# Router logits from the rows themselves, an unsplit first gather, power on GpSimd, twelve load buffers and later second parts of splits

## The chip, the core and the metric

One core of a Trainium2 chip runs one launch of the kernel. The metric is the device time of that launch in microseconds. TensorE (PE) multiplies matrices, VectorE (DVE) and ScalarE (ACT) do elementwise work, GpSimd (POOL) does a little of it, and SyncE (SP) issues the loads. Each engine takes its instructions in the order in which the program lists them and waits on semaphores where data is not ready.

## What is computed

Two layers over 256 tokens of width 1024. Each layer has a token-mixing half (a gated recurrence beside differential attention) and a channel-mixing half: a dense SwiGLU in layer 0, eight experts with two per token in layer 1.

```python
for l in range(2):
    sh1, sc1, g1, sh2, sc2, g2 = split(silu(c) @ ada_w[l] + ada_b[l])
    h = rmsnorm(x, ln1_g[l]) * (1 + sc1) + sh1
    z = h @ w_in[l]
    lru = rg_lru(causal_conv(xr), ...) * gelu(yr)
    att = diff_attention(q, k, v, positions, ...)
    x = x + g1 * (concat([lru, att]) @ w_out[l])
    h = rmsnorm(x, ln2_g[l]) * (1 + sc2) + sh2
    x = x + g2 * (swiglu(h) if l == 0 else moe(h))      # moe: top 2 of 8 by h @ router
return rmsnorm(x, final_g)
```

All of it is float32. Weights are some 420 MB, read once.

## The kernel before

The weights are one stream of chunks of 128x2048 floats (1 MB). `want` and its relatives (L98, L992 to L1021) list the stream; `fetch` (L110) issues the load of the next chunk on SP at the place where the program first needs it. SP runs ahead of the other engines, so a load starts when its buffer is free. There are 10 rotating buffers and, in the experts, `raw2` as an eleventh. For the first 12 expert chunks there is a twelfth, made of two halves from the tags `eh` and `el` (L120).

A product in full precision is made of three fast ones. `split_next` (L138) takes half a chunk, a piece of 128x1024, and makes `wh` (ACT, rounded, L147) and `wl` (DVE, the rest, L148). `refill` (L167) keeps four pieces ready; `quarter` (L158) is one step of work on one piece: `tick()`, `refill()`, then the piece's matmuls. `tick` (L182) is the hand-written order of everything else: `after(n, fn)` puts `fn` n ticks later, in front of that tick's `refill`. `TICKS` (L67) holds the tick of each step of the mixing halves: `setup` (preparation of angles, masks and recurrence constants, L207 on), `scan` and `out` (`lru_scan`, L712; `lru_out`, L728), softmax steps and so on.

In layer 0 `mix_start` (L1047) begins with `queries_keys` (L591), eight quarters, one for each block k of the input; their matmuls are L599 (with `wh`) and L602 (with `wl`). Blocks come in pairs: `prepare_quarter` (L1082) makes a pair ready and lifts `limit`, which lets the next two pieces be split. Setup steps are due at ticks 3, 4, 5, 5, 6 and 11.

The inverse root of the mean square is made by DVE alone from a first guess in integer arithmetic and three Newton steps: `rsqrt` (L476) for the heads, `inv_rms` (L508) for rows, `inv_rms_all` (L1745) at the end.

During the dense half, `ada_sums` (L362) adds up the conditioning rows of layer 1 on DVE, into tiles that POOL clears and gives the bias (`ada_bias`, L372); `ada_row` (L380) sums them over partitions and ACT copies the result.

`route` (L1305) norms both row tiles, transposes them, applies gain and shift, forms the logits, takes the best two, ranks the tokens of each expert and starts the first gather. `gather` (L1451) collects the tokens of an expert by matmuls with 0/1 matrices; it reads normed rows split into `xh` and `xl`. Then experts run by load: places 0 to 2 (j = 0, 2, 3 of the loop in `experts`, L1616) hold up to 128 tokens and use split weights (`glu_unit`, L845), places 3 and 4 (j = 5, 6) up to 96 (`glu_mid`, L921) and the rest (j = 1, 4, 7) up to 64 (`glu_half`, L880); the last two kinds multiply raw chunks in float32 without a split. `scatter` (L1564) brings the results of a large expert back.

Of the kernel before, what the change touches and what calls it, by code (L numbers as in the profile page):

```python
# [39 lines left out]
SCATTER = [1, 1, 1, 6, 1, 1, 5, 2, 2, 2, 2]  # L40
# [22 lines left out]
SHORT = 12  # L63
# [3 lines left out]
TICKS = [{"setup": [3, 4, 5, 5, 6, 11], "steps": STEPS, "rk": [9, 10], "rq": [10, 10], "tk": [10, 11], "tq": [12, 12], "s": [12, 14, 16, 17], "conv": [13, 13], "gate": [14, 15], "decay": 16, "scan": 19, "gelu": 19, "out": [20, 21], "v": 21, "att": [22, 24], "norm": [23, 27], "ada": [12, 12, 12, 15, 15, 16, 19, 19, 20], "fill": [0, 4, 4]}, {"setup": [1, 3, 3, 7, 7, 8, 10], "steps": STEPS, "rk": [9, 9], "rq": [10, 11], "tk": [10, 10], "tq": [11, 12], "s": [12, 14, 16, 17], "conv": [11, 13], "gate": [14, 15], "decay": 16, "scan": 19, "gelu": 19, "out": [20, 21], "v": 21, "att": [22, 24], "norm": [23, 31], "ada": [7, 9, 10, 10, 15, 15, 16, 17, 18], "fill": [1, 1, 3]}]  # L67
# [8 lines left out]
class Kernel:  # L76
    def __init__(self, ctx, tc, a):
# [10 lines left out]
        self.spos = 0  # L88
        self.ready = []
# [20 lines left out]
    def fetch(self):  # L110
# [3 lines left out]
        n = RAW_BUFS + (2 if 0 <= i < SHORT else 1)  # L114
        more = (i if i < SHORT else i - SHORT) % n - RAW_BUFS if i >= 0 else -1
# [3 lines left out]
        else:  # L119
            e[1] = [self.moe.tile([P, PIECE], F32, tag=tag, name="raw", bufs=3) for tag in ("eh", "el")]  # L120
# [86 lines left out]
    def setup(self):  # L207
# [21 lines left out]
        nc.gpsimd.memset(self.ones, 1.0)  # L229
        self.csil = const.tile([P, NK], F32, name="csil")  # L230
# [131 lines left out]
    def ada_sums(self, l, g, half, acc):  # L362
        nc = self.nc
        for i in range(NK if half is None else 4):
            raw = self.load(self.a["ada"][l, g, i // 2 + (0 if half is None else 2 * half), i % 2])
            for j in range(2):
                src = raw[:, j * 1024:(j + 1) * 1024]
                k, out = (i, acc[:, j * 1024:(j + 1) * 1024]) if half is None else (2 * i + j, acc)
                nc.vector.scalar_tensor_tensor(out, src, self.csil[:, k:k + 1], out, op0=ALU.mult, op1=ALU.add)
                yield  # L370

    def ada_bias(self, l, g, half, n, tag):  # L372

        acc = self.work.tile([P, 4 * n], F32, tag=tag, name="sums")
# [133 lines left out]
    def inv_rms(self, *ts):  # L508
# [5 lines left out]
        for t, (v, k, y, u) in zip(ts, r):  # L514
            ss = self.ss[t]
            nc.vector.tensor_scalar(v[:, 0:1], ss[:, 0:1], ss[:, 1:2], D * EPS, op0=ALU.add, op1=ALU.add)
# [1433 lines left out]
```

## Time and profile before

| | us |
|---|---|
| median of 3 runs | 1282.72 |
| lowest, highest | 1280.12, 1283.36 |
| profiled execution | 1281.7 |
| its span on the core | 1279.7 |
| busy: PE, DVE, ACT, POOL | 1225.4, 706.1, 553.7, 15.1 |
| moved by DMA | 424.68 MB, mean 332 GB/s |

The page gives shares over the whole span. The kernel goes through stages that differ in what limits them, so the rows below are taken from single stages: windows of time with the busy time of each engine and the rate of the loads, the chain of work that ended last, and the timeline of a few microseconds.

### The profile page before, as it was taken

What the parts mean: (1) busy time and instruction counts of PE and PEld (TensorE: products, weight loads), DVE (VectorE), ACT (ScalarE), POOL (GpSimd) and SP (SyncE); (2) the same over time, 40 slices, a digit from 0 to 9 for tenths busy, and PEclk for the clock granted to TensorE, in tenths of its full rate; (3) what the DMA queues carried; (4) which work ended last, traced back from release to release, by engine and by line L of the source; (5) the groups of instructions that cost most, each with busy time, mean ns of one, the idle gap of its engine ahead of it and who ended that gap; (6) DMA issues with size and microseconds to landing.
All of it is one profiled execution on the core that took longest, in us unless ns stands there. A gap on an engine that the chain in (4) does not pass through costs nothing.

```text
span 1279.7 us, 19448 instructions
## 1 busy us (share of the span) xinstructions
PE 1225.4 (96%) x7702; PEld 810.8 (63%) x7702; DVE 706.1 (55%) x1095; ACT 553.7 (43%) x812; POOL 15.1 (1%) x28
## 2 busy tenths in 40 slices
PE   6999999999999899999998999999999999999994
PEld 5777799999978678788434888888433333333331
DVE  4878778776577768889205988999301001000102
ACT  3475444444455937788104787777110000010001
POOL 0000100000000000000000000000000000000000
PEclk9999999999999998999999999999999999999998
DMA  9985878887454257889899999999899999799993
GB/s 378 425 353 184 319 259 328 304 303 279 164 218 161 100 197 283 298 335 351 356 427 427 426 426 380 354 352 370 350 426 427 425 413 415 300 377 376 426 427 154
DMA packets 60147, 424.68 MB, mean 332 GB/s; under 512 B 7394, under 2 KB 7658, under 8 KB 8848
## 3 DMA queue, kind: packets, MB, share of 16 engines
q1 hardware_dynamic: 59760, 423.28, 83.5%
q8 instruction: 62, 1.02, 0.3%
q14 instruction: 37, 0.30, 0.1%
q0 software_dynamic: 288, 0.09, 0.0%
HBM read 422.29 MB, written 1.05 MB: 331 GB/s over the span
## 4 chain that ended last, share of the span: by engine, by line
PE 60%; DMA 4%; DVE 4%; ACT 2%; issue 1%; DVEq 0%; ACTq 0%; SPq 0%
PE gps L895 4%; PE ups L895 4%; PE yps L987 3%; PE gps L948 3%; PE ups L948 3%; PE bps L960 3%; PE yps L917 3%; DMA raw<-i_md 3%; PE yps L203 3%; PE yps L202 3%; PE yps L204 3%; PE gps L203 3%; PE gps L204 2%; PE gps L202 2%; PE ups L204 2%; PE ups L202 2%
## 5 line engine op out<-in xcount | busy, mean ns | idle before, releaser
L148 DVE TENSOR_TENSOR wl<-raw,wh 128x1024 fp32r<-128x1024 f32 x344 | 411.4, 1221 | 92.6 <-ACT wh L147 89.2
L147 ACT ACTIVATE wh<-raw 128x1024 fp32r<-128x1024 f32 x344 | 358.9, 1059 | 148.9 <-PE gps L586 46.2
L586 PE MATMUL gps<-hl,wh 128*128 128x256 f32 x384 | 96.5, 283 | 0.7 <-DVE hl L572 0.7
L584 PE MATMUL gps<-hh,wh 128*128 128x256 f32 x384 | 96.6, 284 | 0.4 <-DVE hh L571 0.4
L586 PEld LDWEIGHTS gps<-hl,wh 128*128 128x128 f32 x384 | 73.6, 192 | 1.3 <-DVE hl L572 1.1
L584 PEld LDWEIGHTS gps<-hh,wh 128*128 128x128 f32 x384 | 73.6, 192 | 0.8 <-DVE hh L571 0.6
L906 DVE TENSOR_TENSOR sgs<-sgs,ups 128x512 f32<-128x512 f32 x9 | 6.2, 689 | 121.5 <-PE ups L895 121.5
L917 PE MATMUL yps<-raw,hTs 128*64 128x512 f32 x288 | 68.2, 597 | 4.2 <-DMA raw<-i_md 4.2
L953 DVE TENSOR_TENSOR sgm<-sgm,ups 128x512 f32<-128x512 f32 x6 | 4.1, 688 | 116.7 <-PE ups L948 116.7
L895 PE MATMUL ups<-raw,ef 128*64 128x512 f32 x288 | 65.5, 595 | 1.5 <-DMA raw<-i_mu 1.5
L895 PE MATMUL gps<-raw,ef 128*64 128x512 f32 x288 | 66.3, 598 | 0.0
L588 PE MATMUL gps<-hh,wl 128*128 128x256 f32 x384 | 61.7, 283 | 0.0
L203 PE MATMUL gps<-wl,eh 128*128 128x512 f32 x144 | 57.1, 396 | 2.3 <-DVE wl L148 2.3
L202 PE MATMUL yps<-wh,fh 128*128 128x512 f32 x144 | 58.3, 405 | 0.0
L202 PE MATMUL gps<-wh,eh 128*128 128x512 f32 x144 | 57.3, 398 | 0.0
L202 PE MATMUL ups<-wh,eh 128*128 128x512 f32 x144 | 57.2, 397 | 0.0
L203 PE MATMUL yps<-wl,fh 128*128 128x512 f32 x144 | 57.1, 396 | 0.0
L203 PE MATMUL ups<-wl,eh 128*128 128x512 f32 x144 | 57.0, 396 | 0.0
L204 PE MATMUL gps<-wh,el 128*128 128x512 f32 x144 | 57.0, 396 | 0.0
L204 PE MATMUL ups<-wh,el 128*128 128x512 f32 x144 | 57.0, 395 | 0.0
L204 PE MATMUL yps<-wh,fl 128*128 128x512 f32 x144 | 56.7, 394 | 0.0
L588 PEld LDWEIGHTS gps<-hh,wl 128*128 128x128 f32 x384 | 53.0, 192 | 0.0
(336 smaller groups left out, 2046.3 us busy)
## 6 DMA issues: line engine op xcount, KB each, us to landing
raw<-i_mu SPq DMA_DIRECT2D x96, 1024.0 KB, 8.9
raw<-i_md SPq DMA_DIRECT2D x96, 1024.0 KB, 10.2
raw<-i_mg SPq DMA_DIRECT2D x95, 1024.0 KB, 8.6
raw<-i_ada SPq DMA_DIRECT2D x48, 1024.0 KB, 6.8
raw<-i_win SPq DMA_DIRECT2D x20, 1024.0 KB, 10.2
raw<-i_fg SPq DMA_DIRECT2D x12, 1024.0 KB, 6.5
raw<-i_fu SPq DMA_DIRECT2D x12, 1024.0 KB, 5.5
raw<-i_fd SPq DMA_DIRECT2D x12, 1024.0 KB, 5.1
```

Source lines behind the costliest of these rows:

```text
L147: nc.scalar.activation(wh, raw, AF.Copy)
L148: self.rests.append(lambda: nc.vector.tensor_tensor(wl, raw, wh.bitcast(F32), op=ALU.subtract))
L202: mm(out, lhsT=xh, rhs=wh, start=start, stop=False)
L203: mm(out, lhsT=xh, rhs=wl, start=False, stop=False)
L204: mm(out, lhsT=xl, rhs=wh, start=False, stop=stop)
L584: self.nc.tensor.matmul(out, lhsT=w, rhs=hh[:, k, :], stop=False, start=k == 0 and (len(ks) == NK or m + j == 0))
L586: self.nc.tensor.matmul(out, lhsT=w, rhs=hl[:, k, :], start=False, stop=False)
L588: self.nc.tensor.matmul(out, lhsT=wl[:, j * len(ks) + i, :], rhs=hh[:, k, :], start=False, stop=k == NK - 1 and (len(ks) == NK or m + j == 1))
L895: nc.tensor.matmul(ps[c * HALF:(c + 1) * HALF, :], lhsT=eh[:, k, :], rhs=w[c][i // 2][:, i % 2, :], start=k == 0, stop=k == NK - 1)
L917: self.nc.tensor.matmul(y[n * HALF:(n + 1) * HALF, :], lhsT=hT[:, b, c * HALF:(c + 1) * HALF], rhs=w[n][b // 2][:, b % 2, :], start=i == 0 ...
L948: nc.tensor.matmul(ps[q(2 * c + s), :], lhsT=eh[:, k, q(s)], rhs=ws[w][c][i // 2][:, i % 2, :], start=k == 0, stop=k == NK - 1)
L960: nc.tensor.matmul(bp[q(2 * w + c), :], lhsT=eh[:, k, q(2)], rhs=ws[w][c][i // 2][:, i % 2, :], start=k == 0, stop=k == NK - 1)
```

## The change

Nine things are changed.

1. Layer 1's router: the rows of x are transposed as they are, without the norm; the logits are products of these with router times gain, then scaled by the inverse root and shifted by a row worked out earlier (`router_row`). The first gather reads the normed rows in float32, unsplit, 128 columns wide; `xh` and `xl` are made two and three ticks later. Two of the four conditioning loads in `route` are moved to ticks 1 and 2, the addition to tick 3.
2. Each inverse root: a power of -0.5 on GpSimd and one Newton step.
3. In the experts all chunks go round 12 buffers; the twelfth is a half `raw3` and the tile `xn1` of `core`. The tag `xn` with two buffers becomes two tags, `xn0` and `xn1`; `el` goes from three buffers to two.
4. `refill` issues `wh` of a new piece, then `wl` of the pieces that earlier calls left over; `piece` issues it if it is still missing.
5. `ada_bias` is gone: the first term of each sum writes instead of adding, the bias comes with `mod_row` at tick 20, and `ada_row` adds on DVE instead of copying on ACT.
6. In both layers `"out": [20, 21]` becomes `"out": [19, 21]` in `TICKS`.
7. `SCATTER` has other ticks, and `scatter` handles one half of the columns after the other.
8. `mhalf`, a constant of -0.5, is written at the start on POOL.
9. The cleared half of the slot matrix in `route` is no longer needed.

```diff
-SCATTER = [1, 1, 1, 6, 1, 1, 5, 2, 2, 2, 2]
+SCATTER = [1, 1, 1, 3, 2, 2, 1, 1, 3, 2, 2]
...
-        n = RAW_BUFS + (2 if 0 <= i < SHORT else 1)
-        more = (i if i < SHORT else i - SHORT) % n - RAW_BUFS if i >= 0 else -1
+        more = i % (RAW_BUFS + 2) - RAW_BUFS if i >= 0 else -1
...
-            e[1] = [self.moe.tile([P, PIECE], F32, tag=tag, name="raw", bufs=3) for tag in ("eh", "el")]
+            e[1] = [self.moe.tile([P, PIECE], F32, tag="raw3", name="raw", bufs=1),
+                    self.core.tile([P, PIECE], F32, tag="xn1", name="raw")]
...
     def piece(self, n):
+        if len(self.rests) >= len(self.ready):
+            self.split_rest()
         return [w.rearrange("p (a b) -> p a b", a=n) for w in self.ready.pop(0)]
 
     def refill(self, most=1 + AHEAD):
+
+        old = len(self.rests)
         while len(self.ready) < most and self.spos < self.limit and self.split_at(self.spos * PIECE // RAW):
-            self.split_next()
+            self.split_next(False)
+        for _ in range(old):
+            self.split_rest()
...
-        nc.scalar.activation(row, ps, AF.Copy)
+        nc.vector.tensor_tensor(row, ps, row, op=ALU.add)
...
         for t in ts:
-            r.append([self.small.tile([P, 3], F32, tag=f"iv{t}", name="iv")]
-                     + [self.small.tile([P, 1], d, tag=f"i{n}{t}", name=n) for n, d in zip("kyu", (I32, F32, F32))])
...
+            nc.vector.tensor_scalar(v, ss[:, 0:1], ss[:, 1:2], D * EPS, op0=ALU.add, op1=ALU.add)
+        for v, y, u in r:
+            nc.gpsimd.tensor_tensor(y, v, self.mhalf[:, 0:v.shape[-1]], op=ALU.pow)
+        for v, y, u in r:
+            nc.vector.scalar_tensor_tensor(u, y, y, v, op0=ALU.mult, op1=ALU.mult)
+        for v, y, u in r:
+            nc.vector.scalar_tensor_tensor(y, u, 3.0, y, op0=ALU.subtract, op1=ALU.mult)
+        return [y for v, y, u in r]
...
+        def best(t, y):
+            nc.vector.scalar_tensor_tensor(lg[:, t, :], lps[t], y, self.rbias, op0=ALU.mult, op1=ALU.add)
+            nc.vector.max(top[:, t, :], lg[:, t, :])
+            nc.vector.max_index(idx[:, t, :], top[:, t, :], lg[:, t, :])
+            nc.vector.tensor_copy(idf[:, t, :], idx[:, t, 0:2])
...
+        self.flip(banks, self.x[:, 0, :], 0, 0)
+        run(2)
+        self.flip(banks, self.x[:, 1, :], 1, 0)
+        for i in range(4):
+            copy(0, i, False)
+        for i in range(4):
+            copy(1, i, i % 2)
+        y, = self.inv_rms(1)
+        logits(0)
+        logits(1)
...
+        def parts(t):
+            nc.scalar.activation(xh[t], out[t], AF.Copy)
+            nc.vector.tensor_tensor(xl[t], out[t], xh[t].bitcast(F32), op=ALU.subtract)
+
+        for t in range(NT):
+            self.after(2 + t, lambda t=t: parts(t))
...
-        self.after(1, lambda: gate2(1))
+        for n in range(3):
+            self.after(1 + n, lambda: run(1))
```

## Rows read from the trace of the kernel before

**Rows 1.** Windows: busy us of PE, PEld, DVE, ACT, POOL; clock, DMA share, GB/s.
```profile
760.00:860.00 100.00, 100.00 (x447) 80.86 (x446) 92.87 (x90) 79.25 (x89) 0.00 (x0) 1.00 0.97 368
```
**Rows 2.** Windows of ten microseconds where loads start to follow without a break.
```profile
610.00:620.00 10.00, 10.00 (x47) 4.64 (x48) 2.31 (x4) 1.01 (x2) 0.00 (x0) 1.00 0.61 228
620.00:630.00 10.00, 10.00 (x46) 3.21 (x42) 1.94 (x3) 1.12 (x2) 0.00 (x0) 1.00 1.01 426
...
1150.00:1160.00 10.00, 10.00 (x98) 2.96 (x90) 0.18 (x1) 0.60 (x1) 0.00 (x0) 1.00 0.63 236
```
**Rows 3.** The chain that ended last: start, us, what.
```profile
496.78 5.15 PE gaps L1489 x32
...
663.52 19.04 DMA raw<-i_md
...
1238.51 19.52 DMA raw<-i_md
```
**Rows 4.** Timeline of layer 0's first projection: start, us, engine, line, output<-inputs.
```profile
27.62 2.36 DVE L148 TENSOR_TENSOR wl<-raw,wh 128x1024 fp32r<-128x1024 f32 x2
...
29.73 1.07 PE L602 MATMUL zps<-wl,hh 128*128 128x512 f32 x4
...
29.90 0.16 DVE L252 CAST set<-set 128x2 f32<-128x2 int32 x1
...
33.97 0.28 DVE L405 TENSOR_TENSOR row<-adaps,row 128x128 f32<-128x128 f32 x1
...
34.30 0.39 PE L412 MATMUL colps<-cst,row 128*128 128x4 f32 x2 [1.03 <-DVE row L405]
...
38.19 2.35 DVE L148 TENSOR_TENSOR wl<-raw,wh 128x1024 fp32r<-128x1024 f32 x2
...
39.46 1.20 PE L602 MATMUL zps<-wl,hh 128*128 128x512 f32 x4
...
42.70 0.07 DVE L301 MEMSET set<- 128x8 f32 x1
```
**Rows 5.** Timeline where layer 0's output product begins.
```profile
108.00 1.20 DVE L148 TENSOR_TENSOR wl<-raw,wh 128x1024 fp32r<-128x1024 f32 x1
...
110.92 0.79 PE L202 MATMUL wops<-wh,hh 128*128 128x512 f32 x1 [2.72 <-DVE hh L571]
...
111.51 0.63 PE L203 MATMUL wops<-wl,hh 128*128 128x512 f32 x1
```
**Rows 6.** Timeline: POOL's work, and an inverse root on DVE from first to last.
```profile
34.41 0.10 POOL L666 MEMSET xr<- 128x12 f32 x1 [30.55 <-ACT sincos L270]
...
150.87 1.35 DVE L536 TENSOR_SCALAR xn<-x,y 128x1024 f32<-128x1024 f32 x1
...
485.38 0.21 DVE L516 TENSOR_SCALAR iv<-ss 128x1 f32<-128x1 f32 x1 [0.19 <-ACT junk L505]
...
487.36 0.75 DVE L536 TENSOR_SCALAR xn<-x,y 128x1024 f32<-128x1024 f32 x1
...
1264.61 2.50 POOL L1768 TENSOR_TENSOR o<-x,fg 128x512 f32<-128x512 f32 x2 [68.33 <-DVE x L1535]
```
**Rows 7.** Timeline where layer 1 begins.
```profile
365.37 1.12 ACT L387 ACTIVATE row<-adaps 128x256 f32<-128x256 f32 x3
365.49 0.21 DVE L516 TENSOR_SCALAR iv<-ss 128x1 f32<-128x1 f32 x1 [0.18 <-ACT junk L505]
```
**Rows 8.** Timeline of the routing and of the first expert's start.
```profile
494.14 1.22 DVE L1372 TENSOR_TENSOR xl<-xn,xh 128x1024 fp32r<-128x1024 f32 x1
...
496.38 1.22 DVE L148 TENSOR_TENSOR wl<-raw,wh 128x1024 fp32r<-128x1024 f32 x1
...
501.91 0.48 PE L202 MATMUL gps<-wh,eh 128*128 128x512 f32 x1
...
507.47 4.62 DVE L148 TENSOR_TENSOR wl<-raw,wh 128x1024 fp32r<-128x1024 f32 x4
513.14 1.23 DVE L148 TENSOR_TENSOR wl<-raw,wh 128x1024 fp32r<-128x1024 f32 x1 [1.05 <-ACT wh L147]
```

More of the change, by code (lines that the diff above doesn't have):

```diff
@@ L1235, in layer_mix, with router_row @@
         return out
+    def router_row(self):
+        nc = self.nc
+        ps = self.psum.tile([P, 1], F32, tag="tr", name="rsps")
+        for b in range(NK):
+            nc.tensor.matmul(ps[0:NE], lhsT=self.rout[:, b, :], rhs=self.shift2[:, b:b + 1], start=b == 0, stop=b == NK - 1)
+        col = self.small.tile([NE, 1], F32, tag="rcol", name="rcol", bufs=1)
+        nc.vector.tensor_copy(col, ps[0:NE])
+        ps = self.psum.tile([P, NE], F32, tag="tr", name="rsps2")
+        nc.tensor.matmul(ps, lhsT=col.to_broadcast([NE, P]), rhs=self.ident[0:NE, 0:NE], start=True, stop=True)
+        self.rbias = self.const.tile([P, NE], F32, name="rbias")
+        nc.vector.tensor_copy(self.rbias, ps)
     def norm_part(self, t, n, out):
@@ L1276, in dense @@
         parts = ((0, 0, 256), (0, 1, 256), (1, None, 512))
-        accs = [self.ada_bias(l + 1, g, half, n, f"sums{i}") for i, (g, half, n) in enumerate(parts)]
+        accs = [self.work.tile([P, 4 * n], F32, tag=f"sums{i}", name="sums") for i, (g, half, n) in enumerate(parts)]
         def sums():
@@ L1283, in dense @@
         self.spread(ADA1[:1] + ADA1[1:] * 40, sums())
+        rows = []
+        self.after(20, lambda: rows.extend(self.mod_row(l + 1, g) for g in range(2)))
         for u in range(NU):
@@ L1289, in dense @@
         self.flush()
-        self.rows = [self.pre.tile([P, 512], F32, tag=f"row{g}", name=f"row{g}") for g in range(2)]
-        self.rows.append(self.mod_row(l + 1, 2))
+        self.rows = rows + [self.mod_row(l + 1, 2)]
         out = []
@@ new lines, in ranks @@
+        def ranks(t):
+            nc.vector.scalar_tensor_tensor(rank[:, t, :], rk[:, t, :], 1.0, mem[:, t, :], op0=ALU.add, op1=ALU.mult)
+            self.place_one(rank, 0, t, pl)
+        self.flip(banks, self.x[:, 0, :], 0, 0)
[8 more added lines that the diff above has]
+        logits(1)
+        pl = self.work.tile([P, NT, 2 * P], F32, tag="pl", name="pl0", bufs=1)
@@ L1357, in route @@
[L1357 to L1359 removed]
+        xh = [self.core.tile([P, D], F32R, tag=f"hh{t}", name="xh") for t in range(NT)]
+        xl = [self.core.tile([P, D], F32R, tag=f"hl{t}", name="xl") for t in range(NT)]
+        e = small.tile([P, NT, 2], F32, tag="tope", name="tope")
@@ L1449, in slots, with gather @@
         return pl
[L1451 removed]
+    def gather(self, js, srcs, pl=None):
         nc, work = self.nc, self.work
@@ L1619, in experts @@
         self.junk = "sg"
-        pl = self.slots(True)
-        rank, gate, xh, xl = self.route(out)
+        out, pl, xh, xl = self.route(out)
         self.taken = {}
-        steps = self.gather([0], xh, xl, pl)
-        next(steps)
+        steps = self.gather([0], [[w] for w in out], pl)
         self.split_rest()
```

223 lines of the change are left out of this document (87 added, 136 removed).

## The prediction

> **What bounds the kernel now.** I read the waits of TensorE stage by stage first, then the load rate in windows of ten microseconds, then the timeline at the few places where TensorE waits. Three kinds of stage show. The mixing halves, the dense half and the large experts are held by TensorE; VectorE is close behind it in the large experts, 92.87 us busy of 100 [rows 1]. The small experts j = 1 and j = 7 are held by the loads: the chain ends in load waits of 19.04 and 19.52 us [rows 3]. What sets their end is the last moment at which a load found no free buffer. In the windows 610 to 620 and 1150 to 1160 loads pause (DMA share 0.61 and 0.63); behind them they run without a break at 426 GB/s [rows 2]. So time that TensorE gains ahead of either pause is gained at the end, and one more chunk loaded ahead of a pause is gained as well. The third kind is a handful of joints (start of layer 0, output products, norms, routing) where TensorE waits for VectorE.
>
> **Twelve buffers.** A chunk of 1.049 MB at 426 GB/s takes 2.46 us. The pauses leave 3.9 and 3.7 us of idle loads in those windows [rows 2], so a twelfth buffer has room to fill in each. Before, the twelfth existed only for the first 12 expert chunks, long before either pause. Value: 2 x 2.46 = -4.9. Bounds: -4.9 and 0, the latter if a buffer comes free too late, since later second parts of splits hold raw data a quarter longer. I take -4.9: a quarter of a large expert is shorter than the idle time.
>
> **Later second parts.** In steady work this moves `wl` by one quarter, with two more in hand; I cost it at nothing there, the cover being the pieces split ahead. At layer 0's start there is no cover, since `limit` lets only two pieces be split at a time. Pieces 2 and 3 are split in quarter 2; their `wl` started at 27.62 and TensorE used the first at 29.73 [rows 4]. Now they are issued in quarter 3, after its tick, and that tick (3) holds the setup step from 29.90 to 33.97, 4.07 us. It starts at 27.6, `wl` ends at 27.6 + 4.1 + 1.2 = 32.9, and L602 waits 3.2 us longer. Of that 1.0 comes back, for the column product at 34.30 had waited 1.03 us for an addition behind the same setup step [rows 4]. Net +2.2. It repeats at pieces 4 and 5: the `wl` pair ended at 40.54, the setup steps of tick 5 behind it lasted until 42.77, 2.2 us, and now they come first; L602 moves from 39.46 by 2.2 + 2.2 = 4.4 [rows 4]. Such waits also lower TensorE's clock: behind a wait of 2.72 us a matmul took 0.63 us [rows 5], where the same kind takes 0.48 at 501.91 [rows 8]; I add 1.0 as an estimate for both waits. Sum +5.4, bounds 0 and +7.5. What is queued behind: VectorE's setup steps come earlier, and nobody needs them earlier.
>
> **Output behind the scan.** TensorE waited 2.72 us for the first output part (110.92) [rows 5]. Moved ahead of the `wl` at 108.00, that part is there at about 108. But the second matmul needs this piece's `wl`, and by the point above that is now the one in the place at 108.00, behind three output operations of some 1.8 us together: 108.0 + 1.8 + 1.2 = 111.0, against 111.51. The move is eaten by the deferral: -0.5 in layer 0, 0 taken for layer 1, which has the same order. Bounds -5.4 (both waits vanish) and +1.
>
> **Power on GpSimd.** From 485.38 to 487.36 the old root takes 1.98 us on VectorE [rows 6]. The new one: first operation 0.25, hand-over to GpSimd, power, hand-over back, two operations 0.45. No row shows a power. Its nearest rows are a fill of 0.10 and half of 2.50 for a two-input operation on 512 columns [rows 6]; for a hand-over I use 0.2 (the 0.18 and 0.19 of idle time before a VectorE operation that ScalarE releases [rows 6, 7]). I take 0.4 for the power, as one to four columns are nearer to the fill: 0.25 + 0.2 + 0.4 + 0.2 + 0.45 = 1.5, a gain of 0.48 each; bounds +0.8 gain and 0.4 loss. It counts where VectorE's chain leads: dense start, layer 1 start, end. The head norms lie beside matmuls. At the end it is one chain more: -0.5.
>
> The Trainium skill ("GPSIMD Engine Reference", section 4.1) advises VectorE for elementwise work, GpSimd being about half as fast with two inputs. By that rule a power would cost two small VectorE steps, some 0.4, an estimate from that page, and the sum stays; it says nothing of what a power itself needs.
>
> **No clearing.** GpSimd's three fills of the sums ran while the dense half started, and beside them the norm of 128x1024 took 1.35 us, where 0.75 is usual [rows 6]. Without them -0.6, with the root -0.5: dense start -1.1 (bounds -1.9 and +0.3). In exchange three additions on VectorE take the place of ScalarE's three copies at 365.37 [rows 7]. They stand in VectorE's queue ahead of the root that begins at 365.49; the copies took 1.12 for three [rows 7]; an addition reads one operand more, so I take 1.35 as an estimate, all of which delays the root. Less 0.48: layer 1 start +0.9 (bounds +0.3 and +1.8). The two new row fills at tick 20 lie deep in the dense half.
>
> **The router.** Old: the last root begins at 485.38, the first `wl` of the experts at 496.38, and the first expert's matmuls at 501.91 [rows 6, 8]. New, in VectorE's order from 485.4: two copies 0.7, root 1.5, six small steps per row tile 2.4, norm 0.75, rank and slots 1.1, about 0.7 of waiting for TensorE: first `wl` at 492.6, 3.8 earlier. But the two subtractions `xl` (1.22 at 494.14 and one before it [rows 8]) had filled VectorE's waits; now they stand between the first and the fifth `wl`, +2.4. From there VectorE had no gap until 513.14, where 1.05 us were lost to a `wh` [rows 8]; that goes, as TensorE is ahead. Sum -3.8 + 2.4 - 1.05 = -2.4. The gather (5.15 us for 32 matmuls [rows 3]) has half as many, each in float32; its price lies between half of that and all of it, and VectorE's queue hides the difference. TensorE will reach the experts some 4 us earlier and then wait for the fifth `wl`. The moved conditioning loads and their matmuls fall into that wait. Bounds -5 and +1.5.
>
> **At nothing:** scatter's new order and ticks, the two tags for `xn`, `el` with two buffers. The cover is TensorE's 100 of 100 us [rows 1]; with VectorE at 92.87 that cover is thin, and 0.7 either way is what a lost one would cost. The twelfth buffer's first load waits for `xn1` until tick 2; eleven chunks are ahead of it.
>
> **Sum.** -4.9 + 5.4 - 0.5 - 0.5 - 1.1 + 0.9 - 2.4 = -3.1. The profiled execution took 1281.7, of which 1279.7 are its span; the median of the runs is 1.0 above it, so 1282.7 - 3.1 = 1279.6.
>
> **Rivals.** A: the deferral is harmless in layer 0, because the setup steps run in other gaps of VectorE or the delay is taken up later. For it: one wait for another can hide a delay, as the column product's 1.03 us shows. Against it: order on an engine is fixed. Then 1279.6 - 5.4 = 1274.2; with the output waits gone too, 1269.3. B: the power is dear, a long routine on GpSimd while VectorE stands. Each 0.1 above 0.4 costs 0.1 at the three chains and once more in the router's queue, 0.4 in all. It makes the kernel slower than before from 0.4 + 3.1/4 = 1.2 us a power, and measurably slower from 2.1; at 2.5 it gives 1288.0. For it: nothing shows what a power costs; against it: the short rows of GpSimd. C: the twelfth buffer doesn't do what it says, because deferred `wl` hold the raw chunks until the pause is over; then 1284.5.
>
> **How the numbers follow.** Forecast 0.48, A 0.27, B 0.13, C 0.12. A measurement of this kernel tells 0.3% from no change, 3.85 us: faster is under 1278.9, slower over 1286.6. The forecast's own spread (1276 to 1283) gives 0.22 faster, 0.25 same, 0.01 slower; A 0.25 faster, 0.02 same; C 0.08 same, 0.04 slower; B 0.13 slower. Faster 0.47, same 0.35, slower 0.18. The range of 8 in 10 goes from A with the output waits gone, 1269, to B, 1288.
>
> **What would show it.** Right: in layer 0 two waits of L602 for `wl` of 2.5 to 3.2 us; the column product after the second 4 to 5 us late; an output product whose first matmul starts early and whose second waits for `wl`; the fifth `wl` of the first expert near 506, with TensorE waiting for it; one chunk less to load behind each pause. Wrong: no `wl` waits in layer 0 (A), more than 2 us between a root's first and second VectorE operation (B), or pauses that end with as many chunks to go as before (C).

## The result and the profile after

The changed kernel takes 1295.16 us (1294.13 to 1296.17), the kernel before, beside it on the same chip, 1281.95. The ratio is 1.0099 [1.0086, 1.0112]: slower by 13, where 3 faster was forecast. The profiled execution took 1294.1, 1292.4 of it the span. Set against the trace of before, at points that both have, the 12.7 us of the two spans are made up like this:

| stretch | after less before, us | forecast |
|---|---|---|
| start to the end of layer 1's first projection | +4.5 | +4.7 |
| to the end of layer 1's output product | +4.9 | 0 |
| to the first gather | -0.7 | -3.8 |
| to the first expert's first matmul | +5.7 | 0 |
| rest of that expert (j = 0) | +1.8 | +1.4 |
| j = 1, held by loads | -2.5 | -2.5 |
| to j = 2's first down product | +1.6 | 0 |
| to the end of j = 6 | +0.9 | 0 |
| j = 7, held by loads | -1.3 | -2.5 |
| end | -2.2 | -0.5 |

So the sum of layer 0's joints came out as worked out, and the loss sits between layer 1's output product and its first expert. In the order of the rows ahead of the prediction:

The large experts stand as they did [rows 1]. Windows of the changed kernel (busy us of PE, PEld, DVE, ACT, POOL; clock, DMA share, GB/s):

```profile
776.00:876.00 100.00, 100.00 (x445) 80.64 (x444) 92.24 (x89) 78.87 (x88) 0.00 (x0) 1.00 0.97 378
```

The pauses of the loads are there too [rows 2]; windows of the changed kernel:

```profile
630.00:640.00 10.00, 10.00 (x46) 3.17 (x44) 2.10 (x3) 1.48 (x3) 0.00 (x0) 1.00 0.73 278
...
1165.00:1175.00 10.00, 10.00 (x100) 3.10 (x96) 0.00 (x0) 0.60 (x1) 0.00 (x0) 1.00 0.60 232
```

The chain that ended last still ends in load waits [rows 3], now with one more of them in a row at each end of the chain:

```profile
662.39 15.12 DMA raw<-i_mu
677.53 18.69 DMA raw<-i_md
...
1236.97 17.33 DMA raw<-i_mu
1254.32 18.65 DMA raw<-i_md
```

Timeline of the changed kernel, layer 0's first projection [rows 4]. The three marked matmuls are those with `wl` that wait for the deferred second parts, 2.99 and 2.53 where two of 2.5 to 3.2 were forecast. The third, 2.02, is not the deferral's:

```profile
32.45 1.19 PE L596 MATMUL zps<-wl,hh 128*128 128x512 f32 x4 [2.99 <-DVE wl L148]
...
43.51 1.20 PE L596 MATMUL zps<-wl,hh 128*128 128x512 f32 x4 [2.53 <-DVE wl L148]
...
55.68 1.20 PE L596 MATMUL zps<-wl,hh 128*128 128x512 f32 x4 [2.02 <-DVE wl L148]
```

The kernel before has the same wait for the last pair of pieces, 5.6 us earlier:

```profile
50.12 1.21 PE L602 MATMUL zps<-wl,hh 128*128 128x512 f32 x4 [2.04 <-DVE wl L148]
```

Timeline where the output products begin [rows 5]. The first matmul has lost its wait, the second has got one, in layer 0 (113.48) and in layer 1 (450.25):

```profile
113.48 0.47 PE L208 MATMUL wops<-wh,hh 128*128 128x512 f32 x1
...
116.37 0.75 PE L209 MATMUL wops<-wl,hh 128*128 128x512 f32 x1 [2.42 <-DVE wl L148]
...
450.25 0.49 PE L208 MATMUL wops<-wh,hh 128*128 128x512 f32 x1
...
453.48 0.50 PE L209 MATMUL wops<-wl,hh 128*128 128x512 f32 x1 [2.74 <-DVE wl L148]
```

Timeline of the dense half's start [rows 6]: an inverse root with its power, from 154.04 to the norm behind it at 155.38. That norm still takes 1.17, not 0.75. GpSimd fills a bias row beside it (L333): the new fills are called at tick 20, but a tick only places them in the program, and GpSimd ran the two at 155.45 and 156.85, not deep in the dense half as the prediction has it:

```profile
154.04 0.21 DVE L513 TENSOR_SCALAR v<-ss 128x1 f32<-128x1 f32 x1 [0.19 <-ACT junk L503]
154.34 0.56 POOL L515 TENSOR_TENSOR y<-v,mhalf 128x1 f32<-128x1 f32 x1 [4.80 <-DVE v L513]
...
154.93 0.22 DVE L517 SCALAR_TENSOR_TENSOR u<-y,v 128x1 f32<-128x1 f32 x1 [0.67 <-POOL y L515]
155.19 0.16 DVE L519 SCALAR_TENSOR_TENSOR y<-u,y 128x1 f32<-128x1 f32 x1
...
155.38 1.17 DVE L529 TENSOR_SCALAR xn<-x,y 128x1024 f32<-128x1024 f32 x1
155.45 0.55 POOL L333 MEMSET row<- 128x512 f32 x1
```

Timeline where layer 1 begins [rows 7]: the three additions take 1.35, the number taken for them, and the root behind them starts at 370.80, when they are done:

```profile
369.54 1.35 DVE L390 TENSOR_TENSOR row<-adaps,row 128x256 f32<-128x256 f32 x3
...
370.80 0.20 DVE L513 TENSOR_SCALAR v<-ss 128x1 f32<-128x1 f32 x1
```

The two places that the prediction did not have are in layer 1. Timeline of the changed kernel, between the halves of the output product:

```profile
473.28 1.05 PE L443 MATMUL colps<-cst,row 128*128 128x4 f32 x8
...
474.73 1.22 DVE L148 TENSOR_TENSOR wl<-raw,wh 128x1024 fp32r<-128x1024 f32 x1
475.86 0.16 DVE L445 COPY shift<-colps 128x8 f32<-128x8 f32 x1
476.08 0.55 PE L1238 MATMUL rsps<-shift,rout 128*8 128x1 f32 x16 [1.74 <-DVE shift L445]
...
476.86 0.38 PE L1242 MATMUL rsps<-cst,rcol 8*128 8x8 f32 x2 [0.24 <-DVE rcol L1240]
477.17 2.75 PE L474 MATMUL rowps<-row,cst 128*128 128x512 f32 x4
...
478.93 1.42 PE L208 MATMUL wops<-wh,hh 128*128 128x512 f32 x1
```

`router_row`'s products stand between the column product and the row product. The first needs the shift, whose copy VectorE has behind a `wl`; TensorE stands 1.74 us, and the row product behind it takes 2.75 where it took 1.96 in the kernel before:

```profile
469.43 1.96 PE L471 MATMUL rowps<-row,cst 128*128 128x512 f32 x4
```

Between the slots and the first gather TensorE has the conditioning matmuls that were not moved:

```profile
503.26 1.94 PE L363 MATMUL adaps<-raw,csil 128*32 128x256 f32 x16
505.12 4.04 PE L1520 MATMUL gaps<-pl,xn 128*128 128x128 f32 x32
```

And where the first expert begins [rows 8]:

```profile
509.31 1.07 PE L363 MATMUL adaps<-raw,csil 128*32 128x256 f32 x16
...
513.43 2.35 DVE L1391 TENSOR_TENSOR xl<-xn,xh 128x1024 fp32r<-128x1024 f32 x2
...
515.70 0.42 DVE L367 TENSOR_TENSOR row<-adaps,row 128x256 f32<-128x256 f32 x1
...
516.26 0.77 PE L208 MATMUL gps<-wh,eh 128*128 128x512 f32 x1 [5.88 <-DVE row L367]
516.82 0.63 PE L209 MATMUL gps<-wl,eh 128*128 128x512 f32 x1
```

The first expert product waits 5.88 us, and not for a `wl`: it waits for the addition that empties the moved conditioning sums. They and the first gate sum are in the same bank of the accumulators, the addition is due at tick 3, and both `xl` (ticks 2 and 3) are ahead of it on VectorE. The matmuls behind the wait take 0.63 us each, against 0.39 to 0.40 from 519.32 on.

### The profile page after: what moved, and what is told of

It is laid out like the page before. It is cut to its first block, busy times and chain, and to the rows that moved or that the text cites. A ratio compares the mean times of both kernels' runs of the same rounds, so it can differ in the third digit from the quotient of the medians.

```text
span 1292.4 us, 19431 instructions
## 1 busy us (share of the span) xinstructions
PE 1234.6 (96%) x7714; PEld 814.4 (63%) x7714; DVE 689.3 (53%) x999; ACT 551.9 (43%) x803; POOL 21.0 (2%) x39
## 4 chain that ended last, share of the span: by engine, by line
PE 80%; DMA 7%; DVE 7%; ACT 4%; issue 2%; SPq 0%; POOL 0%; POOLq 0%; ACTq 0%; DVEq 0%
PE gps L889 4%; PE gps L580 4%; PE gps L582 4%; PE gps L578 4%; PE yps L981 3%; PE gps L942 3%; PE ups L942 3%; PE ups L889 3%; PE bps L954 3%; DMA raw<-i_md 3%; DMA raw<-i_mu 3%; PE yps L209 2%; PE yps L210 2%; PE gps L209 2%; PE yps L208 2%; PE ups L209 2%
```

## The experiments

Differences in us between two kernels are given from their medians. Where the kernels were not beside each other on one chip, the difference of the two ratios times 1282 may stand behind it, as "by the ratios". What is read from traces compares one execution of each kernel.

### The four suspects, each alone

The theory was: deferral as predicted, the shared bank about 6, the router's row about 4, the twelfth buffer as predicted.

**e1_bank**: the first gate sum goes into another bank.

```diff
         self.taken = {}
+        self.psum.at["gu"] = 2
```

> The changed kernel with one edit: the gate sum of the first expert takes another bank of the accumulator (bank 6 in place of bank 0), so that it no longer shares one with the conditioning sums whose last addition stands at the third tick. Theory (shared bank): the first gate matmul waited 5.88 us for that addition, behind two subtractions of 1.2 us and four split rests on VectorE; with another bank it starts right behind the conditioning matmuls, near 510.5 instead of 516.3, the fifth wl (now at 522.7) comes next late, and of the 5.9 us some 4 to 5.5 are gained: 1290 to 1291 against 1295.2. Rival (VectorE is the bound there anyway): the wait only moves to the fifth wl, and under 1.5 us are gained: above 1293.7.

1288.95, ratio 1.0059 [1.0037, 1.0082]: 6.2 less than the changed kernel (5.1 by the ratios). Timeline of this kernel:

```profile
510.47 0.51 PE L208 MATMUL gps<-wh,eh 128*128 128x512 f32 x1
...
518.36 0.50 PE L209 MATMUL ups<-wl,eh 128*128 128x512 f32 x1 [1.48 <-DVE wl L148]
```

The first product starts 5.8 earlier. What is late next is the fifth `wl`, as the prediction said of this place, at 1.48 us. In the changed kernel itself this `wl` is made at 522.7, where the prediction had it near 506.

**e2_row**: the two products of `router_row` come behind the first and the second group of the output product's second half.

```diff
-            self.router_row()
+        extra = self.router_row() if l == L - 1 else iter(())
...
+            if t == 0:
+                next(extra, None)
             self.norm_part(t, n, out)
...
         nc.vector.tensor_copy(col, ps[0:NE])
+        yield
```

> The changed kernel with one edit: the two products of the new bias row of the router and their copies are issued behind the first two groups of the output product of layer 1 instead of ahead of it. Theory (TensorE's queue): ahead of it they made TensorE wait 1.74, 0.24 and lowered its clock, 4 us in all from the column products to the output product (8.7 us late there against 4.8 before them); behind it they lie beside work: 3 to 4 us gained, 1291 to 1292. Rival (the output product was waiting for its wl at 478.9 in any case): at most 1 us gained, above 1294.

1291.58, 1.0068 [1.0046, 1.0091]: 3.6 less (4.0 by the ratios). The second half of the output product begins at 475.47 instead of 478.93, but TensorE still stands for the row, at its new place, and the product ends only 0.7 earlier (491.50 against 492.22). Another 1.6 of the difference between the two traces lies at the start of j = 2, where no row is. Timeline of this kernel:

```profile
480.43 0.55 PE L1239 MATMUL rsps<-shift,rout 128*8 128x1 f32 x16 [1.31 <-DVE gain L456]
```

The sum of the row has its bank (the one of tag "tr") from the column product, which VectorE reads late (`gain`).

**e3_whole**: `refill` makes both parts of a split at once, as before.

```diff
-        old = len(self.rests)
         while len(self.ready) < most and self.spos < self.limit and self.split_at(self.spos * PIECE // RAW):
-            self.split_next(False)
-        for _ in range(old):
-            self.split_rest()
+            self.split_next()
```

> The changed kernel with splits issued whole again, wh and wl of a piece together, as in the kernel before. Theory (deferral costs at joints and gains nothing elsewhere): the three waits of layer 0's first projection for wl (2.99, 2.53, 2.02 us) and those of the output product (2.42 in layer 0, 2.74 in layer 1) go: 5.5 at the first and about 2.5 at each of the others, 8 to 10 us together: 1285 to 1287. Rival (deferral pays in the large experts, where VectorE is at 92.87 of 100): part of it is lost again there, under 5 us gained, above 1290.

1283.25, 1.0005 [0.9994, 1.0016]: 11.9 less (12.1 by the ratios). The product of the rotation that follows layer 0's first eight quarters is back at 56.79, where the kernel before has it (62.32 in the changed kernel), the output product begins at 107.96, 5.5 earlier than in the changed kernel and 3.0 earlier than before, so the output move now pays.

**e4_eleven**: the changed kernel with eleven buffers in the experts.

```diff
-        more = i % (RAW_BUFS + 2) - RAW_BUFS if i >= 0 else -1
+        more = i % (RAW_BUFS + 1) - RAW_BUFS if i >= 0 else -1
```

> The changed kernel with eleven buffers for the expert chunks, without the twelfth that is made of two halves. Theory (halves load slower): loads in the two stretches without a break run at 420 GB/s with the halves and 426 before; with eleven whole buffers 426 comes back, and each pause loses one chunk of 2.46 us less some 1.1 us of faster loading: 2 to 3 us slower, 1297 to 1298. Rival (the halves cost what the buffer gains): within 0.7 us of 1295.2.

1303.22, 1.0159 [1.0135, 1.0182]: 8.1 more (7.7 by the ratios). The twelfth buffer works, and is worth more than the 4.9 forecast. That the loads run at 420 GB/s because one buffer is made of halves fell: without that buffer they run at 420 to 422 as well.

### Together, and what is left of the deferral

**e5_three**: the edits of e1_bank, e2_row and e3_whole at once.

> The changed kernel with three edits at once: the other bank for the first gate sum, the router's row issued behind the first two groups of the output product, splits issued whole. Each alone gained 6.2, 3.6 and 11.9 us. Theory (the three lie in different stages, and each gain ahead of a pause of the loads is kept): the sum, 21.7, less up to 3 where VectorE catches up: 1274 to 1276. Rival (the loads become the bound once TensorE is faster): over 6 us of the sum are lost: above 1279.5.

1274.09, 0.9940 [0.9923, 0.9957]: 21.1 less than the changed kernel (20.4 by the ratios); the three alone add up to 21.7. So by the medians these three are separate losses, and what is left of the change is faster than the kernel before. In one stretch two of them meet: from the end of layer 1's first projection to the end of its output product the changed kernel takes 59.42, e2_row 58.86, e3_whole 58.50 and both together 54.57. With second parts deferred the row's new place gains 0.6 there, with whole splits 3.9.

**e6_defer_experts**: e5_three, with the deferral kept for expert chunks.

```diff
-            self.split_next()
+            self.split_next(self.spos * PIECE // RAW < self.first)
+        for _ in range(old):
+            self.split_rest()
```

> As the one with three edits, but the later second parts are kept for the chunks of the experts; only the layers and the dense half split whole. Theory (in steady work the later second part is free): within 1 us of the one with three edits. Rival 1 (it pays there, VectorE is at 92.87 of 100): 1.5 us or more faster than it. Rival 2 (it holds raw chunks a quarter longer, and loads start later): 1.5 us or more slower.

1274.73, 0.9952 [0.9937, 0.9968], e5_three beside it 1274.09: in steady work the deferral is worth nothing, and costs nothing, as costed.

**e7_late_parts**: e5_three, with the split of the normed rows at ticks 8 and 10 instead of 2 and 3, and the conditioning loads one tick later.

```diff
-            self.after(2 + t, lambda t=t: parts(t))
+            self.after(8 + 2 * t, lambda t=t: parts(t))
...
-            self.after(1 + n, lambda: run(1))
+            self.after(2 + n, lambda: run(1))
```

> As the one with three edits, and the two subtractions xl with their roundings move from ticks 2 and 3 to ticks 8 and 10, the last two conditioning loads and their addition from ticks 1 to 3 to ticks 2 to 4. Theory (VectorE's queue sets the first expert's start: the wait of 1.48 us for the fifth wl and the lowered clock behind it, and 1.9 us of conditioning matmuls ahead of the gather): 2 to 4 us faster than the one with three edits. Rival (what is moved only fills other gaps that are as tight): within 1 us of it.

1275.34, 0.9947 [0.9928, 0.9965]: no gain. The 2.4 us of `xl` ahead of the fifth `wl`, which the prediction charged, can be moved out of the way and nothing comes of it. In the trace the first gather comes 2.0 earlier behind the output product than in e5_three (10.24 against 12.24), and the first expert takes 1.9 longer (115.10 against 113.17). That VectorE has this work to do somewhere in the first expert in any case would explain it; no run shows it apart.

**e8_eleven**: e5_three with eleven buffers.

> As the one with three edits (1274.1), but with eleven buffers for the expert chunks. Theory (a chunk ahead of each of two pauses, 2.46 us each): about 4.9 slower, 1278 to 1280. Rival (a buffer is worth more than a chunk, since with the later second parts eleven cost 8.0): 7 us or more slower, above 1281; if the later second parts were to blame for that, it is 5 or less here.

1282.51, 0.9995 [0.9983, 1.0007], 8.4 more than e5_three (7.1 by the ratios). By the traces 3.7 of it lie between the end of j = 0 and j = 2's first down product (103.46 against 99.73) and 2.7 in j = 7 (77.60 against 74.93). The second is about a chunk. The first is one and a half; why was not found.

**e9_no_power**: e5_three with the inverse roots of the kernel before.

> As the one with three edits (1274.1), but with the inverse roots by three Newton steps on VectorE as in the kernel before. Theory (a root is 0.73 us shorter with the power, at four chains): 2 to 3 us slower, 1276 to 1277. Rival (as in the kernel before with the power alone, where nothing was gained): within 1 us of 1274.1.

1277.59, 0.9953 [0.9937, 0.9969]: the power is worth 3.5 (1.7 by the ratios), where -0.5 at three places each, 1.5, was taken. In the traces 0.8 lie between layer 0's and layer 1's first projections (332.09 against 331.30) and 0.8 behind the last expert (16.83 against 16.06), where the roots are. Another 2.8 lie in layer 1's output product (57.33 against 54.57), which no root explains. So 1.6 is what the power itself can be given.

**e10_row_later**: e5_three, with the row's products one group later, when `gain` is long out of the bank.

```diff
-            if t == 0:
+            if (t, n) in ((0, 1), (1, 0)):
                 next(extra, None)
```

> As the one with three edits (1274.1), with the two products of the router's row one group later still, behind the second and third group of the output product. Theory (behind the first group they wait 1.31 us for the gain that shares their bank, and the clock falls): 1 to 2 us faster, 1272 to 1273. Rival (that wait only moves to the next joint, the norm of the last rows): within 0.7 us.

1270.87, 0.9911 [0.9887, 0.9935]: another 3.2 (3.7 by the ratios). The output product ends at 475.25 instead of 480.58, but 4.3 of these 5.3 us are there before it begins, at the end of layer 1's first projection (421.75 against 426.01). From there to the end of the output product it takes 53.50 instead of 54.57, and the first expert begins 1.0 sooner behind its gather. The same stretch gives the row's price where splits are whole: 58.50 with the row at its old place (e3_whole), 54.57 behind the first group, 53.50 one group later, and 52.98 in e12_old_route below, which has no row. So the row cost 5.0 between its old place and the best one tried, and 5.5 against none, the last with the faster pace of e12_old_route's matmuls.

### Where the load buffers lie

In the kernel before, loads without a break run at 426 to 428 GB/s, in the changed kernel and in all its variants so far at 419 to 422. The page's row of rates, 40 slices of the span; of the kernel before run once more, **b_same**:

> The kernel before, unchanged, for a trace of it on this chip. Theory (the rate of the loads without a break belongs to the chip): 419 to 421 GB/s in the windows behind the pauses, where the trace that was read first shows 426, the small experts j = 1 and j = 7 1 to 2 us longer, and the time is that of the kernel before, 1282 within its spread. Rival (the rate belongs to the kernel): 426 again.

```profile
GB/s 379 426 352 188 317 260 326 309 302 275 164 218 161 100 197 286 297 331 361 350 427 427 427 426 368 353 358 367 360 427 425 426 412 414 301 379 371 426 427 159
```

and of the changed kernel:

```profile
GB/s 373 419 292 223 288 306 309 311 297 283 163 192 179 103 195 175 313 336 339 343 419 421 420 419 416 358 364 361 339 419 420 419 419 419 347 369 346 419 421 190
```

b_same took 1281.93, 0.9991 [0.9978, 1.0005]. My guess that the rate belonged to the chip fell with it: on one chip it ran at 426, and variants of the changed kernel at 420. **b_pow**, the kernel before with the power alone (and its constant `mhalf`), has the slow rate too.

> The kernel before with one part of the change alone: inverse roots by a power on GpSimd and one Newton step. Theory (a root takes 1.25 us where it took 1.98, by the changed kernel's trace, at dense start, layer 1's start, the routing and the end, four chains): 2 to 3 us faster, 1279.7 to 1280.7 against 1282.65. Rival (the hand-overs wait behind other work of GpSimd, or matmuls hide the root): within 1 us of the kernel before. Its profile also tells whether 427 GB/s in the stretches without a break belongs to the kernel before or to the chip it ran on: if this chip gives 420 with its loads, it is the chip.

1283.34, 0.9999 [0.9982, 1.0017]: no gain in the median, though its ten runs lie between 1276.8 and 1284.6. What the kernels with the slow rate share is a few new bytes of constants, which move the load buffers behind them. These begin at byte 59136 of each partition in the kernel before, at 59168 in b_pow (`mhalf`) and at 59200 in the changed kernel (`mhalf` and `rbias`, the router's shifted row). So four kernels move them by an unused tile among the constants; it moves every other buffer behind the constants by as much:

```diff
         self.ones = const.tile([P, P], F32, name="ones")
+        const.tile([P, 16], F32, name="pad")
```

**b_pad64**: the kernel before with 64 unused bytes, buffers at 59200.

> The kernel before with nothing but 64 unused bytes per partition among the constants, so that the ten load buffers begin at byte 59200 of each partition, as in the changed kernel, in place of 59136, a multiple of 256. Theory (where the buffers begin sets the rate of the loads): 420 GB/s behind the pauses in place of 426, and 2 to 4 us slower, 1284 to 1286. Rival (the rate comes from something else that the change does, the power among it): 426 GB/s and no change.

```profile
GB/s 376 419 361 200 327 265 325 302 311 256 152 248 134 120 173 320 275 336 361 368 421 421 421 420 366 350 359 373 351 421 420 420 417 414 312 365 387 421 421 152
```

1285.65, 1.0031 [1.0018, 1.0043]: slower by 64 bytes that nobody reads, with the buffers where the changed kernel has them. Above is its row of rates; below that of **a_pad**, the changed kernel with 192 unused bytes, buffers at 59392:

> The changed kernel with 192 unused bytes per partition, so that the load buffers begin at byte 59392, a multiple of 256. Theory: 426 GB/s behind the pauses, 2 to 4 us faster, 1291 to 1293 against 1295.2. Rival (the rate doesn't follow the place): no change.

```profile
GB/s 382 426 291 211 306 304 307 310 298 271 163 207 168 99 195 180 309 335 342 342 419 427 426 425 405 355 354 360 338 424 427 424 422 409 349 369 342 423 426 189
```

1292.24, 1.0079 [1.0062, 1.0096]: 2.9 less than the changed kernel (2.6 by the ratios). **b_pow_pad**, b_pow with 224 unused bytes, buffers at 59392:

> The kernel before with the power alone, and 224 unused bytes per partition that bring the load buffers to byte 59392, a multiple of 256 again (with the power alone it was 59168). Theory (the power's gain was eaten by the slower loads): 426 GB/s, and 2 to 4 us faster than with the power alone, 1279 to 1281. Rival (the power gains nothing in the kernel before, since the clock falls in its routing): within 1 us of 1283.3 with 420 or 426 GB/s.

1278.38, 0.9976 [0.9959, 0.9993]: 5.0 less than b_pow (2.9 by the ratios), with loads at 427; its runs lie between 1274.7 and 1282.9, so the two spreads overlap. **e11_pad**, e10_row_later with 192 unused bytes, buffers at 59392:

> The changed kernel with the other bank, the router's row two groups later, splits issued whole (1270.9), and load buffers at byte 59392. Theory: 426 GB/s, 2 to 4 us faster, 1267 to 1269. Rival: no change. Either way it is a candidate for the fastest.

1271.05, 0.9918 [0.9903, 0.9933]: the rate rises to 425 and the time does not change. So the rate follows the pad in every kernel that was run; that it is the place of the load buffers, and not of another buffer moved with them, is likely and not shown. What it is worth is 3 to 5 us by the medians of three pairs and nothing in the fourth. In the traces it is less where the loads hold the kernel: between the changed kernel and a_pad 0.4 from the end of j = 0 to j = 2's first down product (99.85 against 99.42), and 0.7 in j = 7 (74.97 against 74.29).

### The rest of the change

**e12_old_route**: e11_pad with the routing and the first gather of the kernel before, and no router row (and no `rbias`, so its pad is 224 bytes, for the same 59392).

```diff
-        out, pl, xh, xl = self.route(out)
+        pl = self.slots(True)
+        rank, gate, xh, xl = self.route(out)
+        self.place(rank, 0, 0, pl, slice(0, P))
```

> The fastest version (other bank, router's row two groups later, splits whole, load buffers at byte 59392; 1271.05) with the routing and the first gather of the kernel before: normed rows transposed, logits from them, split gather. Theory (freed of the shared bank and of the row's place, the new router still only moves VectorE's work: the two subtractions fall behind the first wl): within 1 us of 1271.05. Rival 1 (the prediction's sum, 2.4 gained by the new router): about 1273.5. Rival 2 (the new router costs even so): 1269.5 or less.

1264.70 (1260.8 to 1265.2), 0.9858 [0.9832, 0.9884]: 6.3 less than e11_pad (7.7 by the ratios), and the fastest kernel seen. It is not the routing itself: from the end of the output product to the first expert's first down product the two take 44.06 and 44.16. The traces part elsewhere: 1.5 less between the two first projections, dense half included, 0.6 in the output product, 2.9 over the first expert as a whole, 4.2 from j = 2's first down product to the end of j = 6 and 0.9 in j = 7, but 1.0 more from the end of j = 0 to that product of j = 2. Windows of 60 us in the first expert, e11_pad:

```profile
530.00:590.00 60.00, 60.00 (x280) 48.90 (x279) 50.77 (x51) 49.29 (x66) 0.00 (x0) 1.00 0.91 341
```

and e12_old_route:

```profile
530.00:590.00 60.00, 60.00 (x283) 49.29 (x283) 51.52 (x52) 49.62 (x67) 0.00 (x0) 1.00 0.91 343
```

Same clock, no gaps in either, 283 matmuls instead of 280. The groups of TensorE by line, 520 to 600, say the same (busy us, mean ns); e11_pad:

```profile
L205 PE MATMUL gps<-wh,eh 128*128 128x512 f32 x32 | 12.7, 396 | 0.0
```

and e12_old_route:

```profile
L205 PE MATMUL gps<-wh,eh 128*128 128x512 f32 x32 | 12.5, 391 | 0.0
```

From start to start, a matmul of 128x512 takes 229 ns in e12_old_route, b_pow and b_pow_pad, and 233 to 234 in the other kernels. These three have the old routing and the power; e9_no_power (new routing, no power) and the kernel before (old routing, no power) are slow. What in them sets the pace was not found. The distance of `wh` and `eh` in a partition is 45504 bytes in the three and 45728 to 46144 in the others (e9_no_power 46144), but it follows from the same two parts of the change, so it may only go along with them. A kernel that moves one operand alone wasn't tried. The pace also means that b_pow and b_pow_pad differ from the kernel before by more than the power and the place: j = 0 takes 110.3 in both and 111.6 in the kernel before.

**e13_out_old**: e11_pad with `"out"` at ticks 20 and 21, as before.

```diff
-"out": [19, 21]
+"out": [20, 21]
```

> The same fastest version with the first output part at tick 20 again, behind the scan by one tick more. Theory (with whole splits the move gives back the waits of 2.72 and 3.68 us of the kernel before for the first output part): 4 to 5.5 us slower, 1275 to 1276.5. Rival (the wait only passes to the next output part): under 2 us slower, below 1273.

1276.25, 0.9959 [0.9947, 0.9972]: 5.2 more than e11_pad (5.3 by the ratios). From the rotation product behind layer 0's first eight quarters to the output product it takes 54.16, as before (54.13), against 51.17 in e3_whole, and 2.4 of the rest are layer 1's.

## Why the prediction was wrong

**The joints of layer 0 were right.** The deferral was put at +5.4, and the last product of layer 0's first eight quarters is 5.5 late. A single trace is a rough measure here: the kernels with whole splits end these quarters between 51.3 and 55.7, those with deferral between 58.2 and 60.6. With the output move, the dense start and layer 1's start the sum stood at +4.7 at the end of layer 1's first projection, and it is +4.5. The dense start came out at -1.1, as summed, by other shares, which is luck: 5.73 us lie between the root's first operation and the first matmul in the kernel before, 4.64 in the changed one, of which the root gives 0.64, the norm 0.18 instead of 0.6 (the old fills are gone, a new one is in their place) and a cast behind it 0.28 (0.43 for 0.71). The bound of the output move, -5.4 with both waits gone, is what e13_out_old measures, 5.2; that the deferral eats it is what the waits of 2.42 and 2.74 at its second matmuls show. Rival A with the output waits gone was 10.3 below the forecast; e3_whole, which makes that case, is 11.9 below the changed kernel.

**The step that failed is the router's.** Its term of -2.4 counted VectorE's operations in order, and TensorE only through the gather. Two things were left out.

The first is the sentence "The moved conditioning loads and their matmuls fall into that wait". Their matmuls do; the addition that frees their bank does not. I did not look up where the first gate sum lies. It lies in the same bank, so TensorE waits for an addition at tick 3, behind both `xl`: 5.88 us in the trace, and e1_bank, which changes the bank alone, is 6.2 faster. The waiting time of the fifth `wl`, put in its place, is 1.48 when the bank is free.

The second is `router_row`. Its line is in the diff's first item, and it has no term in the sum. Two small products and two copies, placed where TensorE and VectorE hand each other work at every step: +4.9 at the end of that product in the trace, and 5.0 between e3_whole and e10_row_later, which differ there in the row's place alone. By the medians 3.6 are got back by e2_row and 3.2 more by e10_row_later.

What the router was to give, -2.4, did not come either. Up to the first gather, -0.7 is measured where -3.8 was taken. The `wl` at 503.18 comes 8.9 us behind the start of the route's chain at 494.25, where 7.2 was worked out: VectorE stands 1.63 for ScalarE's copies of the transposed rows (496.10) and 0.80 for the second tile's logits (500.31), 2.4 where 0.7 in all was taken. The gather then waits for 1.94 us of conditioning matmuls. Even with bank, row and deferral repaired (e11_pad) it takes 44.16 from the end of the output product to the first expert's first down product, against 44.19 in the kernel before: TensorE comes to the first expert 1.9 earlier, and the way from there takes 1.8 longer.

**The twelfth buffer was right in mechanism.** -2.5 at j = 1, as worked out; then +1.6 up to j = 2's first down product and only -1.3 at j = 7. The +1.6 goes with the clock granted to TensorE where j = 2 begins, behind the load waits. Windows of the kernel before, of the changed kernel and of e1_bank at this place:

```profile
690.00:695.00 5.00, 5.00 (x21) 3.23 (x20) 4.97 (x7) 2.60 (x3) 0.00 (x0) 1.00 1.01 426
...
705.00:710.00 5.00, 5.00 (x18) 2.95 (x15) 4.11 (x5) 2.37 (x3) 0.00 (x0) 0.80 1.01 421
...
700.00:705.00 5.00, 5.00 (x22) 3.36 (x21) 4.97 (x6) 3.43 (x4) 0.00 (x0) 1.00 1.01 421
```

In the changed kernel the clock falls to 0.80 and the way from the end of j = 1 to that product takes 29.59; in the kernel before and in e1_bank it stays at 1.00, and the way takes 27.96 and 28.02. Why it falls in some executions and not in others was not tried. Where it stays, in e1_bank and e2_row, the stretch from the end of j = 0 takes 98.6 and 98.2 against 100.74: 2.2 and 2.5 less, as forecast, with loads at 420. The rate of the loads explains less: an estimate by the rates alone (75 us at 420 instead of 426 GB/s) is 1.1 at j = 7, where a_pad shows 0.7 of the 1.2 that are missing. The rate is no step of the prediction; two constants of 64 bytes together, `mhalf` and `rbias`, were taken as nothing. Moving the buffers on to 59392 gave 2.9 in a_pad by the medians. Rival C is out: e4_eleven and e8_eleven lose 7 to 8.

The Trainium skill ("DMA: Bandwidth & Descriptors", section "How a descriptor splits into AXI transactions") says of reads that a descriptor which does not start at a multiple of 256 bytes begins with a transaction at the boundary below, whose unused bytes still cost beats. The addresses here are those written to. 59136 and 59392 are such multiples, 59168 and 59200 are not, so the direction would agree if the same held for them. For a row of 8192 bytes the page's account would give between one beat in 256 and one transaction in 32 more, an estimate from that page; measured is 6 in 426, 1.4%. Four places are too few to show that the multiple is what counts.

**The power was mis-sized, in both ways.** It takes 0.56 us for one column (0.4 was taken), 1.01 for four, 0.72 for two. Yet the root is shorter than worked out: from its first operation to the norm behind it 1.34 at 154.04 against 1.98 in the kernel before [rows 6], a gain of 0.64 for the 0.48 taken, and at the end 0.78 for 0.5. The hand-overs to GpSimd and back are 0.09 and 0.03 where 0.2 each was taken, which outweighs the dearer power. Rival B, which decides from 1.2 us a power, is out. By the half speed with two inputs that the Trainium skill ("GPSIMD Engine Reference", section 4.1) gives for GpSimd, two small VectorE steps, some 0.4, would be an estimate for the power; the trace says 0.56, and e9_no_power says that leaving the power out costs time all the same.

**The end** gained 2.2, of which 0.78 are the root; 1.45 lie behind the last instruction, where the output lands, and no step of the change reaches there.

**What is left open.** Forecast and result are 15.6 us apart, and the two spans differ by 15.9 more than the column of the forecast does. By the table of stretches these are the row's 4.9, the 3.1 that the way to the gather did not give, the bank's 5.7, 0.4 in the rest of j = 0, 1.6 at j = 2 with the lower clock, 1.2 in j = 7 and 0.9 up to the end of j = 6, less 1.7 at the end and 0.2 at the start. The 0.9 goes with a slower pace of the matmuls (234.3 ns from start to start against 233.3 in the kernel before). Why the pace, the clock at j = 2 and 0.5 of j = 7 are as they are, no run here shows.

## What to carry to other kernels

When work of TensorE is moved next to other work, list the accumulator bank of each sum on either side and the instruction that empties it: here a wait of 5.88 us hung on an addition of 0.42 whose result nobody needed yet. Give every new product a line in the sum, however small, with the hand-over to it and from it; eighteen tiny matmuls cost some 5 us at a joint. When a constant is added, look at where the large buffers behind it begin. And before a difference between two traces is given to a change, look at the granted clock in that stretch: 1.6 us of this case went with it.

## What the runs showed of the hardware

- The rate at which loads of 1 MB run without a break went with the byte at which their buffers begin in a partition: 425 to 428 GB/s at 59136 and 59392, 418 to 422 at 59168 and 59200. The unused bytes that set these places moved the other buffers as well. 64 of them made the kernel before slower by 0.31% [0.18%, 0.43%].
- Matmuls of 128x512 at a granted clock of 1.00 have two paces from kernel to kernel, 229 and 233 to 234 ns from start to start, or 391 and 396 ns of mean duration, with no gap between them. The cause is open. By the stages of the traces it is likely to be worth most of the 6.3 us between e11_pad and e12_old_route.
- A power on GpSimd takes 0.56 us for 128x1, 0.72 for 128x2, 1.01 for 128x4.
- A wait lowered the granted clock for a while. In the changed kernel TensorE is busy 0.38 us of the window 510 to 515, and the clock is 0.74 there, 0.58 from 515 to 520 and 1.00 from 520 to 525. The five matmuls behind the first at 516.26 took 0.63 us each; 0.39 came back at 519.32. At the start of j = 2, behind the load waits, the clock was 0.80 from 705 to 710 in the changed kernel and 1.00 at the same place in the kernel before, in e1_bank and in e2_row.
